# Seven block products in place of eight for a gMLP layer's u and gate columns

## The chip, the cores and the metric

The kernel runs on one core of a Trainium2 chip. The metric is the device time of one execution in microseconds (us), the median of three runs. The engines are named as in the profile: PE multiplies matrices, DVE and ACT work elementwise, POOL is a slower elementwise engine, SP issues most of the DMAs.

## What is computed

The reference is a two-layer encoder block. Layer A is a gated MLP with a spatial mixing, layer B a dilated window attention. Only layer A's mixer is touched in what it computes:

```python
def gmlp_mixer(h, w_in, w_s, b_s, vn_g, vn_b, w_out):      # h 1024 x 1024
    z = h @ w_in                                           # w_in 1024 x 6144
    u, v, g = jnp.split(z, 3, axis=-1)                     # 2048 columns each
    u = jax.nn.gelu(u)
    v = layer_norm(jax.nn.gelu(v), vn_g, vn_b)
    nc = s // A_CHUNK                                      # chunks of 128 rows
    vc = v.reshape(bsz, nc, A_CHUNK, A_HEADS, A_HEAD_DIM)  # 16 heads of 128
    sg = jnp.einsum('hpq,bcqhd->bcphd', w_s, vc) + b_s.T[None, None, :, :, None]
    y = u * sg.reshape(bsz, s, A_WIDTH) * jax.nn.silu(g)
    return y @ w_out                                       # w_out 2048 x 1024
```

Layer B projects to queries, keys, values and a gate, attends in three groups, merges the groups by weights, gates and projects again. Each layer is framed by RMS norms and a residual.

## The kernel before, in words

Every operand of a large product is held as a rounded part (hi) and a remainder (lo), and a product is three matmuls: hi by hi, hi by lo, lo by hi. A "piece" is 128 x 512 of such an operand. `Pieces` (lines 119 to 191) loads a piece into one of three `raw` buffers by a DMA on SP, and `_split` writes hi on ACT (line 162) and lo on DVE (line 164) into one of eight `wt` buffers. Pieces stand in one list, and PE takes and frees them in that order. A list entry of kind "sbuf" is split from a tile that is already in SBUF and needs no load.

All matmuls go through `mm` (line 252). `Plan` keeps a clock that advances with each matmul written, and a heap of functions with due times: what is due is written behind the matmul at hand. So the order of instructions on each engine is fixed by the plan, and at run time each engine works through its own order and waits on semaphores.

Layer A runs in three stages:

- Values (to 202 us): columns v of h @ w_in in four passes c over 512 columns. Eight banks of PSUM are filled, and `v_evac` (line 437) writes gelu(v) to the tile `gv` (128 x 8 x 2048, kept in SBUF) and takes statistics.
- Heads (`for h in range(NH)`, line 669): for each of 16 heads `dense` computes 128 columns of u and 128 of g against all 1024 rows. That is two pieces each for u and g, two halves of the rows, eight blocks of the contraction and three matmuls, 96 matmuls of 128 x 512. The two are multiplied (`us<-us,gs`). `spatial` transposes the head's w_s (`ws_tr`, to `wst`), sums its rows with ones (`ws_sum`), splits the head's values from `gv` (`v_split`, to `vs`), and runs four `mix` steps: four matmuls into a bank psS, two DVE operations into `sg`, and one that writes the gated output over `gv`. The mixes of a head run 3 us apart under the next head's products.
- Output (from 584 us): four passes (two halves of the rows, two of the columns) over 16 steps kt. A step takes two pieces, 128 rows of y^T (split from `gv`, kind "sbuf") and 128 rows of w_out (loaded), and runs 12 matmuls. At a pass's end `out_evac` empties four banks with eight ACT operations, and after the second and fourth pass `post` normalises, adds the residual and transposes the next layer's input.

Layer B follows in 1,200 us. Its merge writes a hi and a lo part into the buffer `cb` that held the weights, and stores them from there (`yd<-cb`).

Of the kernel before, what the change touches and what calls it, by code (L numbers as in the profile page):

```python
# [35 lines left out]
POST_EVERY = ((4.0, 15.0), (3.0, 8.0))  # L36

# [84 lines left out]
class Pieces:  # L122
# [10 lines left out]
    def source(self, raw, nr, lo_pool=()):  # L133


        self.raw, self.nr, self.lo_pool = raw, nr, lo_pool
# [3 lines left out]

    def _load(self):
        kind, fn, _ = self.specs[self.loaded]
        if kind == "dram":
            raw = self.raw()
# [6 lines left out]
    def _split(self):  # L151
# [14 lines left out]
        self.split += 1  # L166

    def pump(self):
        while not self.busy:
            if self.loaded < len(self.specs) and len(self.raws) < self.nr:  # L170
                self._load()
            elif self.split < self.loaded and self.split < self.freed + self.room():
# [7 lines left out]
                if kind != "dram" and ready is not None and not ready() and self.split > self.taken:  # L180
# [20 lines left out]
def encoder_block(ctx: ExitStack, tc: tile.TileContext, x, norm_pre, norm_post, a_w_in, a_w_s,  # L201
# [49 lines left out]
    def mm(o, l, r, start, stop):  # L251
        nc.tensor.matmul(o, l, r, start=start, stop=stop)  # L252
        plan.now += 0.0024 + o.shape[-1] / 2400

    def dmm(o, l, r, start, stop):
        mm(o, l, r, start, stop)
        plan.run()
# [69 lines left out]
    for c in range(4):  # L327
        for k in range(8):
            w_rows(a_w_in, 128 * k, W2 + 512 * c)
    for h in range(NH):  # L330
        w_cols(a_w_in, 128 * h)
        w_cols(a_w_in, 2 * W2 + 128 * h)
# [18 lines left out]
    gvs = ExitStack()  # L351
    gvp = gvs.enter_context(tc.tile_pool(name="gvp", bufs=1, reuse_waits="tile"))
    gv = gvp.tile([P, 8, W2], F32, name="gv")
    bst = gvp.tile([P, 8, 4, 6], F32, name="bst")
    mv = gvp.tile([P, 8, 2], F32, name="mv")
# [27 lines left out]
    xt = [gv[:, i, D:2 * D] for i in range(8)]  # L383
# [4 lines left out]
    def x_square(i):  # L388
        act(gv[:, i, 0:D], xt[i], AF.Square, accum_out=xss[:, i:i + 1])
# [43 lines left out]

    def v_stats(i, c):
        nc.vector.bn_stats(bst[:, i, c, :], gv[:, i, 512 * c:512 * c + 512])

    def v_evac(b, i, c):
        act(gv[:, i, 512 * c:512 * c + 512], b, AF.Gelu_apprx_tanh)
# [49 lines left out]

    for c in range(1, 4):
        bs = [bank(t) for t in ("S", "T", "O", "S", "T", "O", "D", "D")]  # L490
        for k in range(8):
# [9 lines left out]

    bvs.close()
    sps = ExitStack()
# [13 lines left out]


    lnr = {}

    def ln_stats():
        for i in range(8):
            nc.vector.bn_aggr(mv[:, i, :], bst[:, i].rearrange("p c k -> p (c k)"))
        lnr["r"] = rsqrt(mv[:, :, 1], 8, 1.0)

    def ln_apply(i):
        ts(gv[:, i, :], gv[:, i, :], mv[:, i, 0:1], OP.subtract, lnr["r"][:, i:i + 1], OP.mult)

    ln_stats()
    for i in range(8):  # L530
        plan.after(3.0 + 2.2 * i, ln_apply, i)
# [34 lines left out]
    def spatial(h, ug, t0, dt):  # L566
        vs, sg, T = {}, {}, ws.pop(h)
        hc = slice(128 * h, 128 * h + 128)
# [14 lines left out]

        def v_split(e):
            if e == 0:
                vs["v"] = sp.tile([P, 2, 8, P], F32R, name="vs", bufs=1)
                act(vs["v"][:, 0], gv[:, :, hc])
            else:
                tt(vs["v"][:, 1], gv[:, :, hc], vs["v"][:, 0].bitcast(F32), OP.subtract)

        def mix(cc):
# [13 lines left out]
            y = gv[:, :, hc].rearrange("p t (c b) -> p c t b", c=8)[:, 2 * cc:2 * cc + 2]  # L605
            tt(y, g.rearrange("p c (b t) -> p c t b", t=8),
               ug[:, 256 * cc:256 * cc + 256].rearrange("p (c b t) -> p c t b", c=2, t=8), OP.mult)
            if cc == 3:
                done_a.add(h)

        plan.at(t0, ws_tr)
        plan.at(t0 + 0.3, v_split, 0)
        plan.at(t0 + 1.5, v_split, 1)
        plan.at(t0 + 2.5, ws_sum)
        plan.at(t0 + 4.0, ws_load, h + 2)
        for cc in range(4):
            plan.at(t0 + 4.0 + dt * cc, mix, cc)

    def y_a(kt, sh):

        def fn(w):
# [812 lines left out]
```

## Time and profile before

| | before |
|---|---|
| median of three runs (range) | 2014.72 us (2014.46 to 2015.49) |
| the profiled execution | 2017.69 us |
| its span in the trace | 2015.8 us |
| mean granted clock of PE | 0.996 |
| PE busy | 1977.0 us, 10,809 matmuls |
| DVE busy | 1206.8 us |
| ACT busy | 988.8 us |
| POOL busy | 234.7 us |

The profile lists the busy time of each engine, a timeline, the chain of work that ended last, groups of instructions with their mean duration, and DMA issues with the time to landing. A matmul's duration overlaps the next one's, so the cost of one on PE is the distance between two starts and not the duration shown. Idle time of an engine that nobody waits for costs nothing.

### The profile page before, as it was taken

What the parts mean: (1) busy time and instruction counts of PE and PEld (TensorE: products, weight loads), DVE (VectorE), ACT (ScalarE), POOL (GpSimd) and SP (SyncE); (2) the same over time, 40 slices, a digit from 0 to 9 for tenths busy, and PEclk for the clock granted to TensorE, in tenths of its full rate; (3) what the DMA queues carried; (4) which work ended last, traced back from release to release, by engine and by line L of the source; (5) the groups of instructions that cost most, each with busy time, mean ns of one, the idle gap of its engine ahead of it and who ended that gap; (6) DMA issues with size and microseconds to landing.
All of it is one profiled execution on the core that took longest, in us unless ns stands there. A gap on an engine that the chain in (4) does not pass through costs nothing.

```text
span 2015.8 us, 30125 instructions
## 1 busy us (share of the span) xinstructions
PE 1977.0 (98%) x10809; PEld 1695.3 (84%) x10809; DVE 1206.8 (60%) x2890; ACT 988.8 (49%) x2215; POOL 234.7 (12%) x330
## 2 busy tenths in 40 slices
PE   8999999999999999999999999999999999999998
PEld 6888888888888889988888888888888889787876
DVE  6223654455454786236576675675775756867647
ACT  5223333333335554236655656656566566575722
POOL 0000000000000000011021130030211301324032
PEclk9999999999999999999999999999999999999999
DMA  4322222221113346222133241332232322313277
GB/s 155 85 79 74 80 83 88 65 89 52 49 42 119 122 146 194 84 87 67 53 89 92 77 122 49 94 92 74 84 96 71 99 79 76 99 54 99 91 225 266
DMA packets 218881, 193.57 MB, mean 96 GB/s; under 512 B 16795, under 2 KB 192571, under 8 KB 218732
## 3 DMA queue, kind: packets, MB, share of 16 engines
q1 hardware_dynamic: 207932, 178.02, 29.4%
q10 hardware_dynamic: 10800, 13.63, 1.9%
q8 instruction: 85, 1.39, 0.3%
q14 instruction: 64, 0.52, 0.1%
HBM read 162.87 MB, written 40.26 MB: 101 GB/s over the span
## 4 chain that ended last, share of the span: by engine, by line
PE 84%; DVE 7%; DMA 5%; ACT 2%; issue 1%; POOL 1%; SPq 1%; DVEq 0%; ACTq 0%; POOLq 0%
PE psD L252 62%; PE psS L252 8%; PE psO L252 7%; PE psT L263 3%; PE psT L252 3%; DMA cb<-sc 2%; DVE o L270 1%; DMA yd<-cb 1%; DVE wt L164 1%; DVE qs L273 0%; DVE pt L270 0%; DVE xs L974 0%; POOL o L270 0%; DMA raw<-in_a_w_in_dram 0%; DVE gv L273 0%
## 5 line engine op out<-in xcount | busy, mean ns | idle before, releaser
L252 PE MATMUL psD<-hTh,wt 128*128 128x512 f32 x2816 | 911.1, 394 | 0.4 <-DVE qs L273 0.4
L252 PEld LDWEIGHTS psD<-hTh,wt 128*128 128x128 f32 x2816 | 515.5, 188 | 89.6 <-PE psD L252 0.8
L252 PE MATMUL psD<-hTl,wt 128*128 128x512 f32 x1408 | 555.9, 395 | 0.0
L252 PE MATMUL psD<-wt,hTh 128*128 128x256 f32 (+1 forms) x1760 | 356.1, 299 | 3.0 <-DVE wt L164 2.1
L164 DVE TENSOR_TENSOR wt<-raw,wt 128x512 fp32r<-128x512 f32 x316 | 214.0, 700 | 166.6 <-ACT wt L162 165.4
L252 PEld LDWEIGHTS psD<-hTl,wt 128*128 128x128 f32 x1408 | 264.9, 188 | 45.2
L252 PEld LDWEIGHTS psD<-wt,hTh 128*128 128x128 f32 x1760 | 281.5, 190 | 14.8 <-DVE wt L164 3.0
L252 PE MATMUL psD<-wt,hTl 128*128 128x256 f32 (+1 forms) x880 | 263.6, 300 | 0.4 <-DVE hTl L270 0.4
L267 ACT ACTIVATE xs<-xs,st 128x256 f32<-128x256 f32 (+2 forms) x384 | 176.7, 461 | 176.2 <-DVE st L974 175.3
L162 ACT ACTIVATE wt<-raw 128x512 fp32r<-128x512 f32 x328 | 195.4, 624 | 134.5 <-PE psD L252 101.3
L252 PEld LDWEIGHTS psD<-wt,hTl 128*128 128x128 f32 x880 | 167.3, 190 | 5.6 <-DVE hTl L270 1.0
L270 DVE TENSOR_TENSOR pt<-psT,pt 128x512 fp32r<-128x512 f32 (+1 forms) x192 | 115.1, 600 | 85.2 <-ACT pt L267 82.6
L974 DVE CUSTOM_DVE_ANT_0 xs<-psS,bias 128x256 f32<-128x256 f32 (+1 forms) x256 | 95.9, 412 | 58.7 <-PE psS L252 56.4
L252 PEld LDWEIGHTS psO<-pt,vs 128*128 128x128 f32 (+1 forms) x640 | 99.5, 177 | 25.8 <-DVE pt L270 9.2
L164 POOL TENSOR_TENSOR wt<-raw,wt 128x512 fp32r<-128x512 f32 x12 | 15.5, 1291 | 902.9 <-DVE wt L164 832.2
L252 PE MATMUL psO<-pt,vs 128*128 128x256 f32 (+1 forms) x640 | 108.3, 283 | 6.4 <-DVE pt L270 4.9
L252 PE MATMUL psS<-ks,qs 128*128 128x256 f32 x640 | 110.6, 286 | 3.2 <-DVE ks L270 3.2
L270 DVE TENSOR_TENSOR ks<-psD,ks 64x512 fp32r<-64x512 f32 x96 | 66.1, 689 | 79.4 <-ACT ks L267 77.8
L252 PEld LDWEIGHTS psS<-ks,qs 128*128 128x128 f32 x640 | 98.2, 190 | 13.7 <-DVE ks L270 4.1
L900 POOL TENSOR_SCALAR ks<-ks 64x512 fp32r<-64x512 f32 x96 | 60.6, 631 | 411.0 <-ACT ks L267 406.3
L263 PE MATMUL psT<-ident,xs 128*128 128x128 f32 x640 | 103.0, 274 | 4.4 <-ACT xs L267 3.6
L267 ACT ACTIVATE pt<-psT 128x512 fp32r<-128x512 f32 (+1 forms) x192 | 100.0, 521 | 14.2 <-PE psT L263 11.3
(192 smaller groups left out, 2531.9 us busy)
## 6 DMA issues: line engine op xcount, KB each, us to landing
raw<-in_b_w_in_dram SPq DMA_DIRECT2D x160, 256.0 KB, 3.3
raw<-in_a_w_in_dram SPq DMA_DIRECT2D x96, 256.0 KB, 3.1
raw<-in_a_w_out_dram SPq DMA_DIRECT2D x64, 256.0 KB, 2.6
y<-yd SPq DMA_DIRECT2D x56, 256.0 KB, 5.2
cb<-sc SPq DMA_DIRECT2D x64, 192.0 KB, 5.3
vt<-vd SPq DMA_DIRECT2D x16, 512.0 KB, 3.6
vd<-tm SPq DMA_DIRECT2D x64, 128.0 KB, 2.6
yd<-cb SPq DMA_DIRECT2D x28, 256.0 KB, 4.5
```

The lines of the kernel that those rows point to most:

```text
L162: self.nc.scalar.activation(hi, src, AF.Copy)
L164: e.tensor_tensor(lo, src, hi.bitcast(F32), op=OP.subtract)
L252: nc.tensor.matmul(o, l, r, start=start, stop=stop)
L263: nc.tensor.transpose(o, i, ident)
L267: nc.scalar.activation(o, i, f, **k)
L270: (e or nc.vector).tensor_tensor(o, a, b, op=op)
L900: nc.gpsimd.tensor_scalar(place(u, u.k[a][:, 0], o, o + 64, hh), hi.bitcast(F32), 1.0, 0.0, op0=OP.mult, op1=OP.add)
L974: nc.vector.tensor_tensor_reduce(out=o, in0=s_, in1=bi, op0=OP.add, op1=OP.min, scale=1.0, scalar=3.0e38, accum_out=col(0, t))
```

## The change

**Layer A's heads.** Rows and contraction are cut in two, so that h^T has blocks a11, a12, a21, a22, and a head's u and g columns are the two column blocks of the weights: b11, b21 for u and b12, b22 for g. Strassen's scheme in Winograd's form needs seven products in place of eight: on the left a11, a12, a22 and the sums s1 to s4, on the right b11, b21, b22 and the sums t1 to t4. The sums of h are formed once, on DVE and ACT, during the values stage (`form`). s1, s2, s4 get tiles of their own, s3 is written over a21 at the end of that stage. The sums of weights are formed for each head on POOL (`w_sum`) from four loads. A product is 12 matmuls (`form_mm`), a head 84. Partial sums are taken out of the bank x between products (`snap`, ACT) and added again (`tt` on DVE).

**Values and gated outputs.** `gv` is gone. gelu(v) goes through five buffers `vst` to `va` in DRAM. Each head loads its values back into one buffer `vr`, normalises them with eight ACT operations, and splits. The gated output is collected in `ya` and stored in DRAM; the output stage loads its pieces of y from there, through the same three `raw` buffers as w_out. The mixes of a head stand at fixed places between the next head's products; those of the last head come together.

**Layer B.** The merge's hi and lo parts overwrite the groups' outputs and are stored in larger parts 2 us later. Loads of pieces are written 2 us later after a split (`slack`).

```diff
+    def form_mm(b, f, first=False):
+        w = pc.take()
+        for k in range(4):
+            hi, lo = form_of(f, k)
+            c = slice(128 * k, 128 * k + 128)
+            dmm(b, w[:, 0, c], hi, first and k == 0, False, not first)
+            dmm(b, w[:, 0, c], lo, False, False, not first)
+            dmm(b, w[:, 1, c], hi, False, k == 3, not first)
+        pc.free()
...
+    def head(h, mixes):
+        if h + 1 < NH:
+            plan.after(0.8, w_load, h + 1)
...
+        form_mm(x, "a11", True)
+        snap("p1")
+        form_mm(z, "a12", True)
+        tt(u[:, c0], z, g["p1"], OP.add)
+        form_mm(x, "s2")
+        snap("u2")
+        y = bank("O")
+        form_mm(y, "s1", True)
+        form_mm(x, "s3")
+        snap("u3")
+        gate(1, y, "u3")
+        for f in mixes[:2]:
+            f()
+        form_mm(x, "a22")
+        act(u[:, c1], x, AF.Gelu_apprx_tanh)
+        act(u[:, c0], u[:, c0], AF.Gelu_apprx_tanh)
+        for f in mixes[2:3]:
+            f()
+        form_mm(y, "s4")
+        gate(0, y, "u2")
+        for f in mixes[3:]:
+            f()
+        for dt, c in ((0.0, 1), (0.9, 0)):
+            plan.after(dt, act, g[c], g[c], AF.Silu)
+        plan.after(1.4, gated, c1, 1)
+        plan.after(2.4, gated, c0, 0)
+        mix = spatial(h, u, plan.now + 0.5)
+        return [lambda cc=cc: mix(cc) for cc in range(4)]
...
     for h in range(NH):
-        u = sp.tile([P, S], F32, name="us")
-        g = sp.tile([P, S], F32, name="gs")
-        dense(lambda b, hh: act(u[:, 512 * hh:512 * hh + 512], b, AF.Gelu_apprx_tanh))
-        dense(lambda b, hh: act(g[:, 512 * hh:512 * hh + 512], b, AF.Silu))
-        tt(u, u, g, OP.mult)
...
+        mixes = head(h, mixes)
+    plan.after(10.0, lambda: [f() for f in mixes])
...
+    def w_sum(h, B, n):
+        f, x, y = (("t1", "b12", "b11"), ("t2", "b22", "t1"), ("t3", "b22", "b12"), ("t4", "b21", "t2"))[n]
+        B[f] = B["b12"] if n == 2 else fm.tile([P, 512], F32, name="tw", bufs=3)
+        tt(B[f], B[x], B[y], OP.subtract, nc.gpsimd)
...
     def v_evac(b, i, c):
-        act(gv[:, i, 512 * c:512 * c + 512], b, AF.Gelu_apprx_tanh)
+        t = vst[i, c] = vp.tile([P, 512], F32, name="vst", bufs=5)
+        act(t, b, AF.Gelu_apprx_tanh)
+        plan.after(1.2, nc.sync.dma_start, va[4 * c:4 * c + 4, :, i].rearrange("h p d -> p h d"),
+                   t.rearrange("p (h d) -> p h d", h=4))
...
+        def v_load():
+            vs["r"] = sp.tile([P, 8, P], F32, name="vr", bufs=1)
+            nc.sync.dma_start(vs["r"], va[h])
+
+        def v_norm(i):
+            act(vs["r"][:, i], vs["r"][:, i], AF.Identity, scale=lnr[:, i:i + 1], bias=lnb[:, i:i + 1])
...
     def y_a(kt, sh):
-        def fn(w):
-            d = w.rearrange("p a (t q) -> p a t q", t=4)
-            return gv[:, 4 * sh:4 * sh + 4, 128 * kt:128 * kt + 128], d[:, 0], d[:, 1]
-        pc.add("sbuf", fn, lambda: kt in done_a)
+        pc.add("dram", lambda raw: (raw, ya[kt][:, 512 * sh:512 * sh + 512]), lambda: kt in done_a)
...
-    pc.source(raw, 3, lo_pool)
+    pc.source(raw, 3, lo_pool, 2.0)
...
-            if not last:
-                nc.sync.dma_start(yd[u.p][:, :, 256 * k:256 * k + 256], y.bitcast(F32))
+            elif k % 2:
+                plan.after(2.0, store, k)
```

The plan moves instructions at three places that matter below. The first is DVE's order at the turn from one head to the next. Before (`us<-us,gs` multiplies u by the gate, `wst` is the lo part of the head's w_s, which PE needs for `ws_sum`; `t` are its sums):

```order
L270 TENSOR_TENSOR us<-us,gs 128x1024
L270 TENSOR_TENSOR wst<-psT,wst 128x128
L164 TENSOR_TENSOR wt<-raw,wt 128x512 x2
L270 TENSOR_TENSOR vs<-gv,vs 128x1024
L273 SCALAR_TENSOR_TENSOR t_2372<-psT,vgb,bsr 128x128
```

And in the change, from the third mix's last operation to the first product of u with its gate (`u_2477<-psO` is a gate sum, the three rows behind it are the fourth mix):

```order
L288 TENSOR_TENSOR ya<-sg,us 128x2x8x16
L178 TENSOR_TENSOR wt<-wb,wt 128x512
L288 TENSOR_TENSOR u_2477<-psO,u_2477 128x512
L291 SCALAR_TENSOR_TENSOR sg<-psS,vgb,t_2432 128x256
L291 SCALAR_TENSOR_TENSOR sg<-psS,vgb,sg 128x256
L288 TENSOR_TENSOR ya<-sg,us 128x2x8x16
L288 TENSOR_TENSOR wst<-psT,wst 128x128
L288 TENSOR_TENSOR us<-us,u_2522 128x512
```

`wst` stood behind one multiplication; it now stands behind a piece, a gate sum and the fourth mix, and ahead of these behind the other gate sum, three mixes and one more piece. The second place is PE at the beginning of the output stage, with the last head's mixes (psS). Before:

```order
L252 MATMUL psS<-wst,vs 128x256 x4
L252 MATMUL psO<-wt 128x512 x4
L252 MATMUL psD<-wt 128x512 x6
L252 MATMUL psO<-wt 128x512 x2
L252 MATMUL psS<-wst,vs 128x256 x4
```

And in the change:

```order
L270 MATMUL psO<-wt 128x512 x4
L270 MATMUL psS<-wst,vs 128x256 x16
L270 MATMUL psO<-wt 128x512 x2
L270 MATMUL psD<-wt 128x512 x6
L270 MATMUL psO<-wt 128x512 x6
```

The four mixes, which were 12 matmuls apart, are now one block. The third place is SP's queue in the output stage. Before:

```order
L146 DMA raw<-in_a_w_out_dram 128x512 x25
L699 DMA xr<-in_x_dram 128x1024
L146 DMA raw<-in_a_w_out_dram 128x512 x4
L105 DMA x1d<-yo 128x512 x2
L146 DMA raw<-in_a_w_out_dram 128x512 x2
```

And in the change:

```order
L160 DMA raw<-in_a_w_out_dram 128x512
L107 DMA x1d<-yo 128x512
L160 DMA raw<-ya 128x512
L107 DMA x1d<-yo 128x512
L160 DMA raw<-in_a_w_out_dram 128x512
L160 DMA raw<-ya 128x512
L160 DMA raw<-in_a_w_out_dram 128x512
L880 DMA xr<-in_x_dram 128x1024
```

Each load of w_out now has a load of y beside it in the same queue and the same three buffers.

## Rows read from the trace of the kernel before

**Rows 1.** The page: busy times, and the clock granted to PE.

```profile
PE 1977.0 (98%) x10809; PEld 1695.3 (84%) x10809; DVE 1206.8 (60%) x2890; ACT 988.8 (49%) x2215; POOL 234.7 (12%) x330
...
PEclk9999999999999999999999999999999999999999
```

**Rows 2.** The page: the chain that ended last, by engine.

```profile
PE 84%; DVE 7%; DMA 5%; ACT 2%; issue 1%; POOL 1%; SPq 1%; DVEq 0%; ACTq 0%; POOLq 0%
```

**Rows 3.** Busy time by stretch: stretch, length, PE, PEld, DVE, ACT, POOL, clock, DMA.

```profile
206.00:590.00 384.00, 384.00 (x1818) 321.19 (x1817) 198.94 (x336) 132.33 (x194) 0.00 (x0) 1.00 0.22 68
...
675.00:750.00 75.00, 74.34 (x343) 61.03 (x342) 65.89 (x166) 44.73 (x93) 0.00 (x0) 1.00 0.46 144
```

**Rows 4.** The chain in order of time in one head: start, length, what.

```profile
303.24 0.48 PE psS L252 x4
303.72 2.74 PE psD L252 x12
```

**Rows 5.** The same view, end of the values stage, beginning of the heads.

```profile
199.34 1.36 PE psD L252 x6
200.70 0.01 issue
```

**Rows 6.** Groups of instructions in the heads, 206 to 590 us: busy us, mean ns.

```profile
L164 DVE TENSOR_TENSOR wt<-raw,wt 128x512 fp32r<-128x512 f32 x62 | 40.2, 686 | 6.9 <-ACT wt L162 6.9
...
L270 DVE TENSOR_TENSOR gv<-sg,us 128x256 f32<-128x256 f32 x60 | 39.6, 661 | 2.1
...
L162 ACT ACTIVATE wt<-raw 128x512 fp32r<-128x512 f32 x61 | 35.1, 623 | 0.0
...
L273 DVE SCALAR_TENSOR_TENSOR sg<-psS,vgb,sg 128x256 f32<-128x256 f32 x60 | 29.1, 484 | 2.2
...
L270 DVE TENSOR_TENSOR vs<-gv,vs 128x1024 fp32r<-128x1024 f32 x16 | 19.5, 1218 | 0.0
...
L270 DVE TENSOR_TENSOR wst<-psT,wst 128x128 fp32r<-128x128 f32 x16 | 4.5, 284 | 0.0
```

**Rows 7.** Timeline around the end of a product that ACT waits for.

```profile
313.39 0.62 PE L252 MATMUL psD<-hTh,wt 128*128 128x512 f32 x2
...
313.82 0.60 ACT L267 ACTIVATE gs<-psD 128x512 f32<-128x512 f32 x1 [2.99 <-PE psD L252]
```

**Rows 8.** POOL's groups: its operation on 128 x 512.

```profile
L164 POOL TENSOR_TENSOR wt<-raw,wt 128x512 fp32r<-128x512 f32 x12 | 15.5, 1291 | 902.9 <-DVE wt L164 832.2 <-ACT wt L162 69.5 <-POOL ks L900 1.1
```

**Rows 9.** Timeline of POOL and DVE in layer B's merge.

```profile
1037.68 1.43 POOL L270 TENSOR_TENSOR o<-o,cb 128x256 f32<-128x256 f32 x2 [4.08 <-DMA cb<-sc]
...
1052.71 3.00 POOL L270 TENSOR_TENSOR o<-o,cb 128x256 f32<-128x256 f32 x2 [1.85 <-DMA cb<-sc]
...
1053.14 1.28 DVE L164 TENSOR_TENSOR wt<-raw,wt 128x512 fp32r<-128x512 f32 x2
```

**Rows 10.** Timeline of a step of the output stage: split and next load.

```profile
640.79 0.62 ACT L162 ACTIVATE wt<-raw 128x512 fp32r<-128x512 f32 x1
...
641.53 0.69 DVE L164 TENSOR_TENSOR wt<-raw,wt 128x512 fp32r<-128x512 f32 x1
...
642.24 0.33 SPq L146 DMA_DIRECT2D raw<-in_a_w_out_dram  x1
```

**Rows 11.** The tile raw in the output stage (590 to 750 us): landing.

```profile
DMA to landing us min/median/max: 2.6/2.6/2.7
```

**Rows 12.** The tile raw in layer B (800 to 1900 us): landing.

```profile
DMA to landing us min/median/max: 2.9/3.3/7.2
```

**Rows 13.** The page: bytes of the SP queue and its share of 16 DMA engines.

```profile
q1 hardware_dynamic: 207932, 178.02, 29.4%
```

**Rows 14.** Timeline of ACT at the end of an output pass.

```profile
627.71 0.58 ACT L267 ACTIVATE yo<-psD 128x512 f32<-128x512 f32 x1
...
632.03 0.65 ACT L162 ACTIVATE wt<-gv 128x512 fp32r<-128x512 f32 x1
```

**Rows 15.** DMA issues in the output stage: KB, us to landing.

```profile
x1d<-yo SPq DMA_DIRECT2D x8, 256.0 KB, 3.5
```

More of the change, by code (lines that the diff above doesn't have):

```diff
@@ L131, in __init__, with source, places, _there @@
         self.waiting = 0.0
-    def source(self, raw, nr, lo_pool=()):
-        self.raw, self.nr, self.lo_pool = raw, nr, lo_pool
+        self.held = []
+    def source(self, raw, nr, lo_pool=(), slack=0.0):
+        self.raw, self.nr, self.lo_pool, self.slack = raw, nr, lo_pool, slack
+    def places(self):
+        return self.nr - len(self.raws) - sum(t > self.plan.now for t in self.held)
     def add(self, kind, fn, ready=None):
         self.specs.append((kind, fn, ready))
+    def _there(self, n):
+        ready = self.specs[n][2]
+        return ready is None or ready()
     def _load(self):
-        kind, fn, _ = self.specs[self.loaded]
+        kind, fn, ready = self.specs[self.loaded]
         if kind == "dram":
+            if not self._there(self.loaded):
+                self.busy = True
+                self.plan.until(ready)
+                self.busy = False
             raw = self.raw()
@@ L166, in _split @@
         self.split += 1
+        if kind == "dram" and self.slack:
+            self.held = [t for t in self.held if t > self.plan.now] + [self.plan.now + self.slack]
+            self.plan.after(self.slack, self.pump)
     def pump(self):
         while not self.busy:
-            if self.loaded < len(self.specs) and len(self.raws) < self.nr:
+            if (self.loaded < len(self.specs) and self.places() > 0
+                    and (self.specs[self.loaded][0] != "dram" or self._there(self.loaded))):
                 self._load()
@@ L179, in pump @@
                     return
-                if kind != "dram" and ready is not None and not ready() and self.split > self.taken:
+                if ready is not None and not ready():
                     return
@@ L382, in encoder_block @@
     pc.source(lambda: pp.tile([P, 512], F32, name="raw0", bufs=8), 8, lo_pool=(1, 3))
-    xt = [gv[:, i, D:2 * D] for i in range(8)]
+    xt = [pp.tile([P, D], F32, name=f"x{i}") for i in range(8)]
+    xsq = pp.tile([P, D], F32, name="xsq")
     def x_load(i):
@@ new lines, in w_load @@
+    def w_load(h):
+        if pc.split < 32 + 7 * h:
+            plan.after(0.5, w_load, h)
+            return
+        cols = a_w_in.shape[-1]
+        B = {}
+        for f, j, c0 in (("b11", 0, 128 * h), ("b21", 1, 128 * h), ("b12", 0, 2 * W2 + 128 * h),
+                         ("b22", 1, 2 * W2 + 128 * h)):
+            B[f] = fm.tile([P, 512], F32, name="wb", bufs=6)
+            nc.sync.dma_start(B[f].rearrange("p (k n) -> p k n", k=4),
+                              bass.AP(tensor=a_w_in.tensor, offset=a_w_in.offset + j * 512 * cols + c0,
+                                      ap=[[cols, P], [128 * cols, 4], [1, 128]]))
+        plan.after(3.0, lambda: w_sum(h, B, 0))
@@ L489, in encoder_block @@
+    for k in range(4):
+        T = {}
+        for n in range(13):
+            plan.after(3.0 + FORM_STEP * (13 * k + n), form, k, n, T)
     for c in range(1, 4):
         bs = [bank(t) for t in ("S", "T", "O", "S", "T", "O", "D", "D")]
+        if c == 3:
+            plan.after(15.0, w_load, 0)
         for k in range(8):
@@ L500, in encoder_block @@
             pc.free()
+    plan.until(lambda: not any(f in (form, nc.sync.dma_start) for _, _, f, _ in plan.heap))
+    for k in range(4):
+        hi, lo = (t[:, k, 512:1024] for t in (hTh, hTl))
+        act(hi, s3[:, k])
+        tt(lo, s3[:, k], hi.bitcast(F32), OP.subtract)
+    for i in range(8):
+        nc.vector.bn_aggr(mv[:, i, :], bst[:, i].rearrange("p c k -> p (c k)"))
+    lnr = rsqrt(mv[:, :, 1], 8, 1.0)
+    lnb = small.tile([P, 8], F32, name="lnb", bufs=1)
+    stt(lnb, mv[:, :, 0], -1.0, lnr, OP.mult, OP.mult)
     bvs.close()
+    vps.close()
     sps = ExitStack()
@@ L680, in out_mm @@
+    mixes = []
+    for h in range(NH):
+        mixes = head(h, mixes)
+    plan.after(10.0, lambda: [f() for f in mixes])
     def out_mm(b, y, w, t, first, last):
```

161 lines of the change are left out of this document (115 added, 46 removed).

## The prediction

> **What bounds the kernel now.** I began with the busy times: PE is busy 98% of the span and its clock is at the full level, 2.4 GHz, in all 40 slices; DVE stands at 60%, ACT at 49% [rows 1]. The chain that ended last lies on PE for 84% [rows 2]. Then I looked at the stage that is changed. From 206 to 590 us PE is busy all 384 us, DVE 199, ACT 132, POOL not at all [rows 3]. So in the heads each matmul less is time less, as long as the work that comes in its place fits on the other engines. How much a matmul costs is read from the chain in order of time: 12 of 128 x 512 take 2.74 us, 0.228 each, and four of a mix 0.48 us [rows 4].
>
> **What the change removes.** A head falls from 96 to 84 matmuls of this shape, 16 heads by 12 is 192, and 192 x 0.228 = **43.8 us**. The mixes stay, and nothing else is taken from PE. A head on PE then lasts 7 x 2.74 + 4 x 0.48 + 0.2 = 21.3 us, where it was 24.
>
> **Small waits that come in on PE.**
> - End of the values stage. Today PE goes on after 0.01 us [rows 5]. Now gelu(v) of eight banks goes through five buffers, and each is free again only when its store has landed. The nearest store takes 3.5 us to land [rows 15]; banks come every 0.68 us (half of 1.36 [rows 5]). The sixth evacuation can begin some 4.5 us after the first bank, not 3.4, and the next two follow at 0.7 or more. The first product of head 0 takes the seventh bank: **+1.5** (0 to 3). The boundaries inside the stage cost nothing, since a bank is written again eight banks later.
> - `snap` before a product that goes on in the same bank. ACT begins to read 0.43 us after the last matmul's start, 0.20 after its 0.23 us slot, and takes 0.60 [rows 7], so PE could go on 0.85 us later. Between s3 and a22 stand two mixes, 0.96 us, and the other snaps have a whole product, 2.74, to hide in. Head 0 has no mixes yet: **+0.8** once.
> - The last head's mixes stand in one block. There are two banks, and DVE frees one after two operations of 0.48 and goes on with one of 0.66 [rows 6]. The third mix waits 0.7, the fourth 1.1: **+1.8** (1 to 3).
>
> **The other engines in the heads.** DVE's work for a head: seven pieces of 0.69, three sums out of PSUM at about 0.6 (nearest: ACT's 0.60 for such a bank [rows 7]), two gate products 1.2 together (as `vs`, of the same size), `vs` 1.2, four mixes of 0.48 + 0.48 + 0.66, `wst` 0.28 [rows 6]: 15.8, and with two small sums about 16.5 of 21.3 us. ACT has seven pieces of 0.62, three snaps and four gelu and silu operations of 0.60, eight small normalisations at about 0.28 (nearest: `wst`), the hi part of `vs` and two table loads, by estimate 15. POOL has four sums of 1.29, 5.2 us [rows 8]. All fit. What can still hold PE is the order. With the head's start at 0, s3 ends at 13.9, the snap at 14.7, and from there DVE has one unbroken row of work to `wst`: two gate sums, four mixes, two pieces and `wst`, 9.4 us, so `wst` is done at about 24.1. PE asks for it 14 matmuls into the next head, at 21.3 + 3.3 = 24.6. The margin is half a microsecond.
>
> What fills it is seen in layer B: two POOL operations that take 1.43 us together take 3.00 when two of DVE's splits (1.28 us) run in their time [rows 9]. One engine stood still for the other. POOL's sums for a later head begin when their loads land and buffers come free, which by the order is around 14 to 20 us of a head, in DVE's unbroken row. One whole sum in DVE's way makes 1.29 - 0.5 = 0.8 us a head, none makes 0. I take half: 0.4 x 15 = **+6** (0 to 12). The Trainium skill ("SBUF — State Buffer", Who interferes with whom) says that a DVE instruction with two SBUF inputs and a POOL instruction that reads SBUF share a port, and that the one that starts first has it for the whole instruction; the rows above agree in size. By that rule taken at its full length all four sums stand against DVE's splits and products, which have two such inputs.
>
> **The output stage.** PE's step kt is 12 matmuls, 2.72 to 2.74 us. It now needs two loads per step through three `raw` buffers. A buffer's cycle: the load lands after 2.6 [rows 11], ACT begins the split, DVE ends it 1.43 us later (640.79 to 642.22), and the next load is issued 0.02 after that [rows 10]: 4.05 us, a third of it 1.35 a piece, **2.70 a step against 2.74**. It fits by nothing. So every delay of a split or a load stays lost until the lead is used up. The lead is eight pieces already split, about 11 us. Against it stand:
> - three pass ends, where ACT empties banks from 627.7 to 632.0 and splits wait some 2.7 us each [rows 14]: 8 us;
> - six loads of 512 KB in the same queue. 178 MB take 29.4% of 2015.8 us [rows 13], so 512 KB take 1.75 us: 10.5 us, of which I count half, because a third of the queue's time is free;
> - `post` in the second half: DVE is busy 65.9 of 75 us [rows 3], of which 38 are splits. A split waits 0.3 us on average, a third of it reaches a piece: 0.1 x 64 = 6.
>
> That is 19 against 11: **+8**. Below: 0, if loads that lie side by side keep 2.6 and bursts are caught up. Above: with a landing of 3.0 a step takes 2.97, 64 x 0.23 = 15 more: 23.
>
> **At no cost.** The sums of h (52 steps 1.9 us apart) run in the values stage, where DVE and ACT are mostly idle and nothing on PE waits for them until the heads. Value loads are issued long before use and hidden by the mixes' late place; if they came late, the mixes would wait on PE. In layer B the matmuls keep their order exactly; the later stores free the weights' buffers earlier and hold the outputs longer. I expect within 2 us either way.
>
> **Sum**: -43.8 + 1.5 + 0.8 + 1.8 + 6 + 8 = **-25.7**. The profiled execution of 2017.69 us would be 1992.0. It lies 3.0 above the median, 2014.72, from which the forecast is **1989.0**.
>
> **Rivals.**
> - *All hidden.* The loads hold 2.6, `wst` comes in time: -43.8 + 4.1 = -39.7, **1975**. For it: DVE and ACT have 20 to 30% free and no raw load of the output stage takes over 2.7 today. Against it: both margins are below a step's noise.
> - *The port.* Two of POOL's sums fall in DVE's row in each head: 2 x 1.29 - 0.5 = 2.1 us by 15, 32 in place of 6: -43.8 + 4.1 + 32 + 8, **2015**, no change; with a third, slower. For it: the 3.00 us above. Against it: most of DVE's row reads PSUM, where nothing of the kind shows.
> - *Slower through the raw ring.* Place: SP's queue in the output stage. With y and w_out loads landing after 3.5 us, as the stores beside them do [rows 15], a step takes (3.5 + 1.45) / 3 x 2 = 3.30: 64 x 0.56 = 36, plus the 8: 44. -43.8 + 4.1 + 6 + 44 = +10, **2025**. It decides from a landing of 3.2 us on: then 64 x 0.36 = 23, plus 8 and 10 make 41, the gain. For it: raw loads in layer B land after 3.3 in the middle and 7.2 at most [rows 12]. Against it: those have smaller rows, and the same load of w_out takes 2.6.
> - *The change does not do what it says.* The matmuls are 192 fewer in the order, so only a part could fail: PE waits in each head on a snap or a mix that I hold for hidden. One microsecond a head more gives 2005.
>
> **Chances.** The forecast with its own spread (1979 to 1998): 0.55. All hidden (1971 to 1979): 0.25. A wait in the heads, 1998 to 2010: 0.07. The port in full (2010 to 2020, half of it slower): 0.06. The raw ring: 0.07. About 0.2%, 4 us, is what a measurement here can tell from no change, so faster means below 2010.7. That makes faster 0.87, same 0.03, slower 0.10. The range is 1971 to 2003: it takes in the first two cases and half of the third, some 8 in 10 and a little over.
>
> **What would show it.** A head in the profile after should last about 21.7 us, with PE's waits on `wst` of 0 to 1 us, none on the snaps but in head 0. In the output stage PE should wait on `wt` splits late, in the third and fourth pass, about 8 us in all, and the chain there should run through raw loads. At the end of the values stage there should be one idle stretch of 1 to 2 us behind an evacuation. I would be wrong in the sizes if the output stage showed no wait or tens of microseconds, and wrong in the mechanism if PE waited in the heads for ACT or for a value load.

## The result, and the profile after

The changed kernel takes **2045.8 us** (median of 4 runs, 2045.4 to 2046.2), the kernel before 2015.1 (4 runs). The ratio is 1.0153 (95% interval 1.014 to 1.0165): **30.7 us slower**, where 25.7 us less was forecast and 2003 was the upper end of the range. The profiled execution has a span of 2043.6 us, 27.8 more than before.

The page of the changed kernel, busy times and granted clock, then SP's queue, then the chain by engine; they answer to [rows 1], [rows 13] and [rows 2]:

```profile
PE 1962.9 (96%) x10617; PEld 1665.1 (81%) x10617; DVE 1325.6 (65%) x3051; ACT 1108.5 (54%) x2455; POOL 332.9 (16%) x394
...
PEclk9999999999989999999999999999999999999999
...
q1 hardware_dynamic: 235068, 219.97, 35.4%
...
PE 68%; DVE 14%; DMA 9%; ACT 4%; issue 3%; SPq 0%; POOL 0%; ACTq 0%; DVEq 0%
```

The 192 matmuls are gone. PE's share of the chain fell from 84% to 68%, and DVE's and DMA's have about doubled: PE now waits. The clock, at its full level in all 40 slices before, stands lower in one of them, from 562 to 613 us. SP's queue carries 42 MB more.

The busy times by stretch (stretch, length, PE, PEld, DVE, ACT, POOL, clock, DMA) answer to [rows 3]. The first row is fifteen heads, the second the second half of the output stage:

```profile
231.00:579.00 348.00, 329.96 (x1529) 268.67 (x1528) 262.82 (x418) 223.67 (x391) 81.35 (x52) 0.99 0.37 115
700.00:775.00 75.00, 64.42 (x275) 48.98 (x274) 55.39 (x140) 37.91 (x76) 0.00 (x0) 0.95 0.61 194
```

Before, PE had no idle time in the heads. Now it stands still for 18 of 348 us there, and for 10.6 of 75 us in the output stage. No engine is full in either stretch: these are waits for order and for landings, not for a bound of work.

Where the time went is read from instructions that every version has. Of the kernel before, the tiles `wsr` and `yo` (duration in ns, least, middle and largest, then the first and the last start in us). The first row is the transpose of a head's spatial weights, 16 of them, which ends the head's products; the others empty the banks at the ends of the four output passes: the first psD is the end of pass 1, the first psS of pass 2, the last psO of pass 3, the last psS of pass 4:

```profile
L263 PE MATMUL psT<-ident,wsr x16: 270/270/270, 223.7 to 583.9; 128*128 128x128 f32 x16
...
L267 ACT ACTIVATE yo<-psD x6: 581/588/600, 627.7 to 764.5; 128x512 f32<-128x512 f32 x6
L267 ACT ACTIVATE yo<-psO x4: 590/596/608, 629.9 to 721.1; 128x512 f32<-128x512 f32 x4
L267 ACT ACTIVATE yo<-psS x4: 580/590/600, 671.2 to 766.6; 128x512 f32<-128x512 f32 x4
...
L267 ACT ACTIVATE qs<-psD x96: 577/593/602, 871.4 to 1881.5; 64x512 fp32r<-64x512 f32 x96
```

The same rows of the changed kernel:

```profile
L281 PE MATMUL psT<-ident,wsr x16: 270/270/272, 230.6 to 579.0; 128*128 128x128 f32 x16
...
L285 ACT ACTIVATE yo<-psD x6: 577/581/587, 634.7 to 797.4; 128x512 f32<-128x512 f32 x6
L285 ACT ACTIVATE yo<-psO x4: 582/588/600, 637.4 to 745.6; 128x512 f32<-128x512 f32 x4
L285 ACT ACTIVATE yo<-psS x4: 585/591/597, 684.3 to 799.5; 128x512 f32<-128x512 f32 x4
...
L285 ACT ACTIVATE qs<-psD x96: 579/592/602, 907.0 to 1911.1; 64x512 fp32r<-64x512 f32 x96
```

| stretch | before | after | difference | by the prediction's terms |
|---|---|---|---|---|
| start to the first transpose (values, head 0) | 223.7 | 230.6 | +6.9 | -2.7 + 1.5 + 0.8 = -0.4 |
| first to last transpose (15 heads) | 360.2 | 348.4 | -11.8 | -41.1 + 6 = -35.1 |
| last transpose to the end of pass 1 | 43.8 | 55.7 | +11.9 | |
| pass 2 | 43.5 | 49.6 | +6.1 | |
| pass 3, to the last psO | 49.9 | 61.3 | +11.4 | |
| pass 4, to the last psS | 45.5 | 53.9 | +8.4 | |
| these four together | 182.7 | 220.5 | +37.8 | 1.8 + 8 = +9.8 |
| to the first `qs` of layer B | 104.8 | 107.5 | +2.7 | 0 |
| first `qs` to the end | 1144.4 | 1136.6 | -7.8 | 0, within 2 |
| span | 2015.8 | 2043.6 | +27.8 | -25.7 |

The heads did become shorter, by 0.8 us each instead of 2.3. The output stage gave back three times that. Layer B, from which nothing was expected, gained.

The end of pass 1 is ACT's mark, and ACT is late there itself. PE's first matmul of pass 2 starts at 632.09 us, 53.1 behind the last transpose, where it was 45.3 before (629.17): 7.8 of the 11.9 are PE's. In the rest ACT stands at a split whose load has not landed, with the full bank behind it in its order.

What PE waits for in the changed kernel: engine and line, what it waited for, us in total, times, longest. The first answer covers 200 to 580 us, the second 580 to 800:

```profile
PE psT L270 <- DVE wst L288: 15.1, 12, 1.8
PE psT L633 <- DMA vrow<-in_a_vnorm_b_dram: 5.0, 1, 5.0
...
PE psD L270 <- ACT psD L285: 9.1, 3, 4.9
...
PE psS L270 <- ACT vs L285: 2.8, 1, 2.8
```

**The heads.** The chain in order of time through one head (start, length, what), the answer to [rows 4]:

```profile
436.15 1.80 DVE wt L178
...
440.03 0.29 DVE wst L288
440.37 0.39 PE psT L270
...
462.84 0.39 PE psT L270
```

From one product with `wst` to the next, 440.37 to 462.84, are 22.47 us, not 21.3. The chain reaches PE over DVE's `wst`, the place that the prediction named. A split of DVE that takes 0.69 alone takes 1.80 in it. The timeline of the same head shows what stands beside it (POOL's operations on tw and wb are the sums of the weights):

```profile
454.55 1.30 POOL L288 TENSOR_TENSOR tw<-wb 128x512 f32<-128x512 f32 x1 [17.15 <-DVE ya L288]
455.93 2.24 POOL L288 TENSOR_TENSOR tw<-wb,tw 128x512 f32<-128x512 f32 x1
458.13 1.74 POOL L288 TENSOR_TENSOR wb<-wb 128x512 f32<-128x512 f32 x1
...
455.39 1.01 DVE L288 TENSOR_TENSOR ya<-sg,us 128x256 f32<-128x256 f32 x1
...
458.62 1.80 DVE L178 TENSOR_TENSOR wt<-wb,wt 128x512 fp32r<-128x512 f32 x1
```

Each of the two engines is slower where the other runs. DVE's split, begun inside the sum of 458.13, takes 1.80 in place of 0.69 and ends 0.55 behind that sum; the product of 455.39, begun inside the first sum, takes 1.01 in place of 0.66 and also ends 0.55 behind it. One of POOL's sums takes 2.24, where the one ahead of it took 1.30. That is the sign of [rows 9], inside the heads. It is no wait for the sums' results: from 231 to 560 us neither DVE nor ACT has a wait on POOL. The Trainium skill ("SBUF — State Buffer", Who interferes with whom) has DVE instructions with two SBUF inputs and POOL instructions that read SBUF exclude each other; the trace agrees, with 1.1 us more on one split.

**The output stage.** The chain in it, the answer to [rows 10]:

```profile
653.66 4.50 DMA raw<-ya
...
664.23 2.67 DMA raw<-ya
...
667.01 0.64 ACT wt L176
...
667.67 0.70 DVE wt L178
...
668.39 2.63 DMA raw<-in_a_w_out_dram
```

The chain no longer lies on PE. It goes from load to split to load: the buffer ring is the bound. A turn with a landing of 2.6 or 2.7 takes 4.1 to 4.2 us (664.23 to 668.39), as the prediction has it, and then PE's step is about held. But not every load lands after 2.6. The tile raw in three stretches of this stage, 590 to 640, 640 to 690 and 690 to 750 us, the answer to [rows 11]:

```profile
DMA to landing us min/median/max: 2.6/2.9/3.3
...
DMA to landing us min/median/max: 2.6/3.0/4.5
...
DMA to landing us min/median/max: 2.4/3.2/5.1
```

The rows hold only the loads whose landing the trace has. Pass 2 takes 49.6 us, 3.10 a step; by the prediction's formula this is a landing of 3.2, a little over the middle of 3.0, since a late load of 4.5 us holds the whole ring. In the last two passes, where ACT's emptying of the banks and `post` come in as well, the loss per pass is larger. PE's longest waits there are for ACT to empty a bank, 9.1 us in three. ACT takes splits and emptyings in one order: at the end of pass 3 it stands 1.5 us at a split for a load, begins the bank at 739.66, and PE, which waits for that bank, goes on at 740.90 after 3.3 us.

### The profile page after: what moved, and what is told of

Read it like the earlier page. It is cut to its first block, busy times and chain, and to the rows that moved or that the text cites. A ratio compares the mean times of both kernels' runs of the same rounds, so it can differ in the third digit from the quotient of the medians.

```text
span 2043.6 us, 30630 instructions
## 1 busy us (share of the span) xinstructions
PE 1962.9 (96%) x10617; PEld 1665.1 (81%) x10617; DVE 1325.6 (65%) x3051; ACT 1108.5 (54%) x2455; POOL 332.9 (16%) x394
## 4 chain that ended last, share of the span: by engine, by line
PE 68%; DVE 14%; DMA 9%; ACT 4%; issue 3%; SPq 0%; POOL 0%; ACTq 0%; DVEq 0%
PE psD L270 50%; PE psO L270 8%; PE psS L270 5%; DVE wt L178 4%; PE psT L281 3%; DMA raw<-in_a_w_out_dram 3%; DVE sg L291 3%; PE psT L270 2%; ACT wt L176 1%; DMA raw<-ya 1%; DVE ya L288 1%; DMA toep<-vec 1%; DVE o L288 1%; DMA raw<-in_b_w_in_dram 1%; DMA vr<-va 1%
## 5 line engine op out<-in xcount | busy, mean ns | idle before, releaser
L270 PE MATMUL psD<-hTh,wt 128*128 128x512 f32 x2176 | 722.3, 396 | 3.7 <-ACT u L285 3.6
L270 PEld LDWEIGHTS psD<-hTh,wt 128*128 128x128 f32 x2176 | 401.1, 189 | 72.2 <-ACT u L285 4.5
L270 PE MATMUL psD<-hTl,wt 128*128 128x512 f32 x1088 | 433.3, 398 | 0.0
L270 PE MATMUL psD<-wt,hTh 128*128 128x256 f32 (+1 forms) x1760 | 360.6, 301 | 9.6 <-ACT psD L285 4.9
L270 PEld LDWEIGHTS psD<-hTl,wt 128*128 128x128 f32 x1088 | 205.3, 189 | 33.4
L285 ACT ACTIVATE ks<-psD 64x512 fp32r<-64x512 f32 x96 | 57.1, 594 | 80.6 <-PE psD L270 79.1
```

The source lines that it names most:

```text
L270: nc.tensor.matmul(o, l, r, start=start, stop=stop, skip_group_check=more)
L285: nc.scalar.activation(o, i, f, **k)
```

## Experiments

Theory, after the traces were read: three buffers for two loads a step cost the output stage some 30 us, DVE's order with POOL's sums some 15 in the heads, the row load before head 0 some 5. Rivals: the DMA queues are the bound in the output stage, whatever the buffers; the head is simply longer in all its parts; the sums themselves have no part in the wait.

### Six buffers for the output stage

The loads of the output stage get a pool of their own, which is opened when the heads' tiles are gone. The order of the plan stays.

```diff
-        pc.source(raw, 3)
+        orp = ors.enter_context(tc.tile_pool(name="orp", bufs=1, reuse_waits="tile"))
+        pc.source(lambda: orp.tile([P, 512], F32, name="rawo", bufs=6), 3)
...
```

> The changed kernel with six buffers in place of three for the loads of the output stage, in the same order of the plan. Theory (the ring): a piece costs a third of landing, split and reissue, so three buffers set the step of the output stage at 3.1 us and more; with six the step goes back to 2.72 to 2.8 us, the passes to about 44 us, and the time falls by 22 to 33 us, to 2013 to 2024. Rival (the DMA engines): two loads a step saturate the transfers, more buffers only queue more, landings rise from 3 to about 6 us, and the time falls by less than 6 us.

Measured: 2014.8 us against 2015.3 before, ratio 0.9994 (0.9985 to 1.0003): 31 us less than the changed kernel. The tile `yo`, the ends of its passes, and behind the dots the landing of the six buffers' loads:

```profile
L285 ACT ACTIVATE yo<-psD x6: 581/586/600, 625.4 to 762.8; 128x512 f32<-128x512 f32 x6
L285 ACT ACTIVATE yo<-psO x4: 585/591/600, 628.1 to 719.0; 128x512 f32<-128x512 f32 x4
L285 ACT ACTIVATE yo<-psS x4: 588/596/600, 668.6 to 765.0; 128x512 f32<-128x512 f32 x4
...
DMA to landing us min/median/max: 2.5/3.6/7.5
```

Passes 2 to 4 take 43.2, 50.4 and 46.0 us, the times of before. And the landing did not become shorter: it is 3.6 in the middle and 7.5 at most, longer than with three buffers. So the DMA engines were not the bound. What was short was the number of loads under way, and here the longer landing costs nothing, since enough of them are. The rival falls.

### The ring alone, in the kernel before

The other way round: the kernel before, with its eight products, gets only the gated outputs through memory and the second load per step.

```diff
+            nc.sync.dma_start(ya[h], vs["y"])
...
-        pc.add("sbuf", fn, lambda: kt in done_a)
+        pc.add("dram", lambda raw: (raw, ya[kt][:, 512 * sh:512 * sh + 512]), lambda: kt in done_a)
```

> The kernel before, eight products and gv as they were, with one part of the change alone: gated outputs are stored in DRAM and loaded for the output stage through the three raw buffers. Theory (the ring): the output stage alone grows from 2.72 to 3.1 to 3.5 us a step, 20 to 32 us more, 2035 to 2047. Rival (the output stage is slow in the changed kernel because it begins with no lead after the new heads): less than 12 us more.

Measured: 2046.7 us, ratio 1.015 (1.0135 to 1.0165), +30. The tile `yo` of this kernel:

```profile
L276 ACT ACTIVATE yo<-psD x6: 578/582/586, 634.4 to 798.1; 128x512 f32<-128x512 f32 x6
L276 ACT ACTIVATE yo<-psO x4: 587/592/598, 637.1 to 745.7; 128x512 f32<-128x512 f32 x4
L276 ACT ACTIVATE yo<-psS x4: 584/588/597, 683.7 to 800.2; 128x512 f32<-128x512 f32 x4
```

Passes 2 to 4 take 49.3, 62.0 and 54.5 us, within 0.7 of the changed kernel's. One part of the change, with no matmul removed, costs as much as the whole change lost. Taking it out and putting it in agree: -31 and +30. It is within the 20 to 32 that the theory gave, and the rival falls: this kernel comes to the output stage from the old heads.

### `ws_sum` 2.5 us later

PE's product with `wst` is moved back in the head, so that DVE's row of work is through when PE asks.

```diff
-        plan.at(t0 + 2.5, ws_sum)
+        plan.at(t0 + 5.0, ws_sum)
```

> The changed kernel with the sums of w_s written 2.5 us of the plan later, so that PE asks for the lo part of w_s at about 26 and not 24.5 us of a head. Theory (a wait at one place): DVE is only late at this place, the 15 us that PE waits for it go, and nothing takes their place: 11 to 16 us less, 2030 to 2035. Rival (DVE bounds the heads): the wait moves to the next mixes or gate sums, and the time changes by less than 4 us.

Measured: 2029.5 us, ratio 1.0073 (1.0058 to 1.0088): 16.3 less than the changed kernel. No wait on `wst` is left, and 15 heads take 331.0 us in place of 348.4. The chain of a head:

```profile
450.87 0.11 PE psT L281
...
452.80 2.72 PE psO L270 x12
...
458.44 2.80 PE psO L270 x12
...
465.01 2.79 PE psD L270 x12
...
472.47 0.11 PE psT L281
```

From transpose to transpose are 21.60 us, all of it on PE: this is the head that the prediction put at 21.3. The 15 heads take 22.07 each on average: waits of 4.6 us for ACT's `u`, in six places, are left. DVE's work is the same as before the edit, so it was one place in the order that held PE, and not the amount of work.

### POOL's sums left out

The four sums of weights per head become a memset of the same tile, so that POOL reads nothing. The sums t1 to t4 are left out of the computation.

```diff
-        tt(B[f], B[x], B[y], OP.subtract, nc.gpsimd)
+        nc.gpsimd.memset(B[f], 0.0)
```

> The changed kernel with POOL's four sums of weights a head replaced by writes of zeros, which read nothing; the products t1 to t4 are left out in that way. Theory (the port): DVE's splits and gated outputs of 1.0 to 1.8 us go back to 0.7, DVE reaches the lo part of w_s about a microsecond earlier, and the 15 us of PE's waits fall to 0 to 5: 9 to 16 us less, 2030 to 2037. Rival (DVE's own row is too long): its long operations stay as they are and the waits stay over 10 us: less than 4 us.

Measured: 2026.7 us, ratio 1.0057 (1.0042 to 1.0072), 19 less than the changed kernel, somewhat more than expected. The wait on `wst` is gone though PE's order is untouched, and 15 heads take 328.4 us. DVE's splits from 231 to 560 us (ns, least, middle, largest), first in the changed kernel:

```profile
L178 DVE TENSOR_TENSOR wt<-wb,wt x56: 674/686/1798, 239.6 to 551.3; 128x512 fp32r<-128x512 f32 x56
```

and with POOL's sums left out:

```profile
L178 DVE TENSOR_TENSOR wt<-wb,wt x56: 659/685/702, 238.6 to 530.7; 128x512 fp32r<-128x512 f32 x56
```

The long splits are gone. So POOL's sums make `wst` late, by standing against DVE's operations. Both edits remove the same wait; the two together were not tried. The edit takes away most of POOL's time along with its reads (a write of zeros takes 0.53 us, a sum 1.3 and more), so that by itself it does not tell a shared port from another cause; the ends of DVE's operations 0.55 us behind those of the sums speak for the port.

### The norm's rows later

The transpose of the value norm's rows waits for a load that stands in SP's queue behind the last value store. It is put 12 us into head 0 in place of 2.

```diff
-    plan.after(2.0, vgb_tr)
+    plan.after(12.0, vgb_tr)
```

> The changed kernel with the transpose of the value norm's weights (its load stands behind eight stores in SP's queue) 10 us of the plan later. Theory: the 5 us that PE waits for that load at the beginning of head 0 go, and with them the 6.8 us at half clock that begin 10 us later, worth 3.4: 5 to 9 us less, 2037 to 2041. Rival: ACT, which still has evacuations and the parts of s3 to do, holds head 0's first snap instead: less than 3 us.

Measured: 2042.5 us, ratio 1.0139 (1.0122 to 1.0156), 3.3 less than the changed kernel and less than expected. The wait of 5.0 us is gone and the first transpose comes at 225.3 us in place of 230.6, 5.3 sooner; the half clock behind the wait is gone too (1.00 from 200 to 250 us in place of 0.93). The rival has a part in it: PE now waits 1.2 us for each of ACT's snaps `p` and `u` in head 0, where it waited 0.7 for `u`. In the profiled executions the gain lasts: the ends of the four passes come 4.9 to 5.7 us sooner and the span is 2038.8 us in place of 2043.6. The medians are 3.3 apart, and the four times of this kernel lie between 2040.3 and 2044.6, so that the gain is known only as some 3 to 5 us.

### Layer B's merge alone

The kernel before, with the changed merge and store of layer B's outputs and nothing else: hi and lo parts are written over tiles of `o`, two pieces are stored at a time, and `cb` is only read.

```diff
-            y = fin["y"][:, :, 256 * k:256 * k + 256] if last else c[:, 0:2]
...
+                yh, yl = o[1].bitcast(F32R), o[0].bitcast(F32R)
...
-                nc.sync.dma_start(yd[u.p][:, :, 256 * k:256 * k + 256], y.bitcast(F32))
...
+            elif k % 2:
+                plan.after(2.0, store, k)
```

> The kernel before with the changed merge of layer B alone (hi and lo over the groups' outputs, stored in larger parts 2 us later), without the later loads. Theory: the 6 us by which layer B is shorter after the change come from this part, since the next weights no longer wait for a store: 5 to 8 us less, 2007 to 2010. Rival: they come from the later loads (slack), and this part alone stays within 3 us of before.

Measured: 2007.5 us against 2016.7, ratio 0.9957 (0.9942 to 0.9971): a gain of 9.2. What the merge's operations on the tile `o` waited for (us, times), first in the kernel before:

```profile
  DMA cb<-sc: 90.4, 25
```

and with the changed merge:

```profile
  DMA cb<-sc: 51.6, 11
```

Before, a buffer of `cb` also held the result until its store had landed, so the next unit's load of `cb` began late. In the chain of layer B (900 to 1850 us) that load falls from 3.9% to 1.0%. The prediction saw both sides, the weights' buffers free earlier and the outputs held longer, and held them for about even.

### Three edits together

Six buffers, the late `ws_sum` and the late rows in one kernel.

> The changed kernel with the three edits together: six buffers for the output stage's loads, the sums of w_s later, the transpose of the norm's weights later. If they are separate waits, their gains add: 31 + 16 + 3, 1993 to 1998, which beats the kernel before by some 18 us. If one hides behind another, 2000 to 2008.

Measured: **1993.8 us** against 2016.7, ratio 0.9885 (0.9871 to 0.99). It beats the kernel before by 23 us and the changed kernel by 52; the single gains make 31.0 + 16.3 + 3.3 = 50.6, so they add within the noise. This is the change as it was meant, and it is near the forecast of 1989.0, for a kernel that is not the one the forecast was for.

### Two more edits, a miss

On top of the three: the value loads are issued on ACT's queue, out of SP's order, and the last head's four mixes go out 3 us apart.

```diff
-            nc.sync.dma_start(vs["r"], va[h])
+            nc.scalar.dma_start(vs["r"], va[h])
...
-    plan.after(10.0, lambda: [f() for f in mixes])
+    for cc in range(4):
+        plan.after(10.0 + 3.0 * cc, mixes[cc])
```

> The three edits, and the heads' loads of values issued from ACT's queue in place of SP's, and the last head's mixes 3 us of the plan apart. Theory: in the last two heads the value load stands in SP's queue behind a load for the output stage that waits for a buffer, which costs PE 3 us a head on vs and on the snap behind it, and the block of mixes costs 1.4: together 6 to 10 us less than the three edits alone, 1986 to 1991. Rival: the value loads are late for another reason (the buffer vr itself), and only the mixes' 1 to 2 us go.

Measured: 2004.5 us, ratio 0.9939 (0.9922 to 0.9956): 11 us worse than the three edits. PE waits 20.3 us in the heads, in four pieces of up to 8.8, for ACT's `u`. The chain of the first head shows why:

```profile
222.14 18.23 DMA vr<-va
```

From the issue of the load on ACT's queue to its use pass 18.23 us, and 11.83 in a second such head (at 340.14). ACT takes its instructions in order, so with the first normalisation of this value tile the snap `u` waits too, and PE for the snap. Why it took so long stays open: the first issue alone took 5.47 us, where the middle one took 0.33, and the landings that the trace has on this queue are 3.4 to 3.5. The 15 heads take 348.2 us in place of 330.8; the stretch from the last transpose to the end of pass 4 gives 7.0 back (184.0 in place of 191.0), which leaves the loss.

### The spaced mixes alone

The three edits, with the last head's mixes 14, 17, 20 and 23 us behind its end, the loads back on SP's queue.

```diff
-    plan.after(10.0, lambda: [f() for f in mixes])
+    for cc in range(4):
+        plan.after(14.0 + 3.0 * cc, mixes[cc])
```

> The kernel with the three edits (six buffers of their own, late ws_sum, late transpose of the norm's rows), plus one: the last head's four mixes go out 14, 17, 20 and 23 us after its end, one at a time, where they went out together after 10 us. Theory (the step that was put at 1.8 us is a wait of the PE for the last head's value load): in the trace of the three edits the PE waits there 2.50 us for ACT's vs, 0.88 for DVE's vs, 1.03 and 0.39 for sg, 4.8 in all, and the clock falls to its half level right behind; with the mixes spaced these waits go and the output stage's first pass ends 5 us sooner after the last transpose of the spatial weights: 1987 to 1990 us. The kernel with five edits, whose mixes were spaced as well, then lost its 11 us to the other edit alone, the value loads on ACT's queue. Rival (the spacing itself was what cost the kernel with five edits its time, because the last head's gated output reaches memory later and the output stage's loads stand behind it): 1994 us or more, with waits of the PE in the first pass of the output stage.

Measured: 1993.5 us against 2015.5, ratio 0.9889 (0.9872 to 0.9905): as the three edits, 1993.8, and not the 1987 to 1990 of the theory. The waits for `vs` are gone, as it has it; but a new wait of 3.7 us for ACT's split of a weight tile has come in pass 1. The chain there:

```profile
590.96 8.11 DMA rawo<-in_a_w_out_dram
```

The last gated output is stored later, at 589.31 in place of 579.37; the first loads of the six buffers stand behind it in SP's queue and go out six at once, and the first lands after 8.11 us. That fits the rival, and the new wait just cancels the gain. But the later store is not shown to be the whole cause: in the three edits the first of these loads went out at 593.13 and was split from 598.90 on, no sooner than here (599.09), and PE, which had stood still before, did not need it yet. As to the run before, its mixes were spaced too, though from 10 us on, and the trace of that run has the output stage 7.0 us shorter: its loss lies in the heads, with the loads on ACT's queue.

## Why the prediction was wrong, step by step

The direction was wrong. By its own steps:

- **The matmuls, -43.8.** Right in count and nearly in size. Where nothing waits, a head takes 21.60 us on PE, 2.41 less than the 24.01 of before, so 38.6 in place of 43.8 for 16 heads. The head was put at 21.3, with 2.74 us a product; five of the seven take 2.79 to 2.81.
- **The end of the values stage, +1.5.** No such wait. The bank was free in time. Instead PE waited 5.0 us for the norm's rows, a load whose place in SP's queue, behind the last value store, the prediction did not look at. The change had moved stores into that queue, and each queue that a step is moved past was to be counted.
- **Head 0's snap, +0.8.** PE waits there 0.7 us for `u`. That is right by luck in part: with the wait for the norm's rows taken away, ACT's snaps cost 2.4.
- **`wst`, +6 (0 to 12).** Right in place, in cause and in the rows it was read from; wrong in size. It measures 15.1 in waits and 16.3 in time. The margin of 0.5 us was nearly right: without the sums `wst` is done at 447.37 us in one head and used at 448.13. A head lost 1.0 us, between the half sum of the forecast, 0.4, and the 2.1 of the rival "the port". Half a sum a head in DVE's way was a middle between two ends, with nothing in a row that spoke for it; the prediction's own timing put the sums into DVE's unbroken row, and in the head shown all four run there (454.55 to 461.56, the row from 452.12 to 462.78).
- **The output stage, +8 (0 to 23).** This is the step that failed: the landing that was put into the ring. The formula holds nearly: landing plus 1.45, by two thirds, gives 2.97 us a step for the middle landing of pass 2, and 3.10 was measured. The warning in it, that 2.70 against 2.74 "fits by nothing", was right. Wrong was the landing that was put in. 2.6 us was read where one load a step is under way [rows 11], and was kept for two loads a step. It measures 2.9 to 3.2 in the middle and up to 5.1. The lead of eight pieces holds through pass 1, where PE waits for no piece; from pass 2 on it is gone, and each late load and each late split is lost for good, as the prediction says of such a ring. The price is the "tens of microseconds" that were named as what would refute the sizes: 31.0 us by taking it out, 30 by putting it in alone. The rival "slower through the raw ring" had the place and the mechanism, and was given a chance of 0.07; at its point of decision, a landing of 3.2 us, its sum for this stage is 23 + 8, the 31 that was measured. Its evidence against, that the same load of w_out takes 2.6, came from a stage with half the loads; its evidence for, 3.3 us in layer B [rows 12], came from a stage with a mix of loads and was the nearer row.
- **The last head's mixes, +1.8 (1 to 3).** The two banks cost what was put on them or less: PE waits 0.7 and 0.4 us for `sg`. What was not in the sum is the last head's value load, for which PE waits 2.8 and then 0.9 us on `vs`; then the clock falls. PE comes to pass 2 7.8 us late in all, and with six buffers the stretch up to the end of pass 1 is still 7.5 us over that of before. The load (issued at 581.47) stands in SP's queue behind one of the output stage (581.10), and the load ahead of it, for the head before, held PE for 2.9 us through a snap of ACT. The prediction named "PE waited in the heads for ACT or for a value load" as what would refute its mechanism; here it did.
- **Layer B, within 2.** Wrong to the good side: 7.8 us less in the changed kernel, 9.2 alone. The buffers that come free earlier were named, and put at nothing.
- **The clock** was not in the sum at all. It is told below.

Over the stretches of the table the misses are +7.3 before the heads' first transpose, +23.3 in the heads, +28.0 in the output stage, +2.7 behind it and -7.8 in layer B: 53.5, which is 27.8 + 25.7. The three edits, each aimed at one of the first three, gave back 52.

## What to carry to other kernels

A buffer ring's rate is buffers over (landing + use), and the landing to put in is the one under the new load, not the one read today: where the rate so found meets the consumer's step with no margin, count the ring as the bound and add buffers first, since a longer landing costs little while enough loads are under way. Where an operand's tile is due half a microsecond before it is asked for, move the asker, and only then look at what makes the tile late. A load or store put in a new place on a queue is to be followed to whatever else stands in that queue, SP's and ACT's alike: three of the misses here, the norm's rows, the last value load and the value loads on ACT, were of that kind.

## What the runs showed of the hardware that was not expected

**The clock falls behind a wait.** The busy times by stretch of the changed kernel, the granted clock third from the end of a row:

```profile
200.00:225.00 25.00, 19.23 (x70) 14.52 (x69) 12.69 (x37) 8.63 (x17) 7.12 (x6) 0.86 0.62 176
...
475.00:500.00 25.00, 23.19 (x103) 18.75 (x102) 18.20 (x29) 14.67 (x27) 6.71 (x5) 0.93 0.38 111
...
575.00:600.00 25.00, 20.26 (x86) 16.19 (x86) 18.50 (x35) 12.96 (x25) 0.00 (x0) 0.87 0.41 137
```

In the kernel before, the clock is 1.00 from 200 to 800 us. Here it goes to its lower level, 1.2 GHz, behind waits of PE: at 200 to 225 us it had waited 5.0 for the norm's rows, at 575 to 600 4.7 in four pieces for the last head's values and mixes. Such a long wait is not needed: from 475 to 500 PE's only wait is one of 1.8 us, for `wst`. The other eleven waits on `wst`, none of them longer, left the clock at 1.00; why this one did not stays open. The chain behind the first of these waits shows the price:

```profile
208.75 1.15 PE psD L270 x2
209.91 4.95 PE psO L270 x12
```

Twelve matmuls take 4.95 us in place of 2.72, and two ahead of them 1.15 in place of 0.46: with the wait of 5.0 it makes 7.9 in this chain. Taking the wait away gave less, 5.3 us by the first transpose, since ACT's snaps, which it had covered, then held PE for 2.4. A wait on PE is to be priced with what comes after it, and with what it covers.

**Five of a head's seven products take longer.** In the head of the late `ws_sum`, twelve matmuls of a11 and a12 take 2.75 and 2.72 us, those of s1 to s4 2.80 or 2.81, and a22 2.79 (465.01 in the chain). It is 0.3 us a head. The tile is not the cause, since a22 lies in the tiles of h itself and s3 was written over a21, and the weights' values are not, since with the sums of weights at zero a product s1 takes 2.80 as well. What makes the difference stays open.

**With more loads under way each lands later.** Three buffers: 3.0 us in the middle over the whole output stage, with a step of 3.10 and more. Six: 3.6 us, with PE's own step of 2.72. It costs nothing only while split pieces lie ready: with the spaced mixes the first of six loads landed after 8.11 us, and PE waited 3.7.
